# One turn of a background job placed 300 instructions ahead, Strassen sums on VectorE, and a planner's clock with new costs, in a hybrid decoder layer

## The chip, the cores and the metric

The kernel runs on one core of a Trainium2 chip. What counts is the device time of one execution in microseconds (us), as the median of several runs. Times inside the kernel come from one profiled execution.

## What is computed

One decoder layer on 1032 tokens (1024 of a prompt and 8 single ones of running sequences), width 1024, all in fp32:

```
x = x + 1/2 * SwiGLU_1(RMSNorm(x))                 # FFN1, inner width 2816
n = RMSNorm(x);  p = n @ w_in_mix                  # one projection, columns split among heads
mix = concat(window_attention(p), gated_DeltaNet(p)) @ w_out_mix
x = x + mix
x = x + 1/2 * SwiGLU_2(RMSNorm(x))                 # FFN2
y = RMSNorm(x)
```

`swiglu(x, w_in, w_out)` is `(silu(gate) * up) @ w_out`, with gate and up the two halves of `x @ w_in`. The DeltaNet group has four heads; each needs, in chunks of tokens, the inverse of a unit lower triangular matrix, and then a scan over the chunks that carries a state of 128 x 128. New caches and states are outputs beside `y`.

## The kernel before

The activations lie with the model's width on partitions: 8 tiles (`KT`) of 128 rows by 1032 tokens. TensorE (PE) multiplies in a fast format, so every fp32 product is three: high part by high part, high by low, low by high. A weight or an activation is split into `hi` (a cast on ScalarE, ACT) and `lo` (a subtraction on VectorE, DVE, or on GpSimd, POOL). `mm3` (L325 to L327) is one such triple. Tokens go in three chunks of 344, or in four quarters of `HW` = 258; two quarters make a half `p`.

**Stages.** *FFN in* uses a Strassen-like scheme: `w_ops` and `x_ops` build seven weight and seven activation operands out of four blocks by sums and differences, and `product` (L515 to L517) multiplies each pair into one of three PSUM banks. `x_ops` makes four 128x1032 sums (`t1`, `t2`, and two in place in `x`) and splits seven operands into `xhi` and `xlo`. The first `HEAD` = 4 column blocks f of FFN1 are done by `ffn_head` without that scheme, out of the raw x times the norm's gain (`xg`): there 1/rms (`rs`) of each token is multiplied in when the two PSUM banks are evacuated, so PE can start before the norm is known. *FFN out* (`ffn_out`) is plain `mm3`. The *token mix* (`mix_in`, `mix_out`) projects, convolves, does attention and DeltaNet, and ends in the product with `w_out_mix` in two passes, the second of which adds into x, squares and feeds the norm of FFN2.

**Norms.** `prepare(p, ...)` handles a half: `squares` (FFN1), then `rstd`, which lets PE sum over partitions (rows `ones,acc`), does a reciprocal square root by an integer guess and three Newton steps in small DVE operations (`nv`, `rsqt`, `rsqy`), spreads the result on a diagonal (`t`, three DVE operations) and lets PE broadcast it (rows `t,ones`); then 8 norm products on DVE per quarter (SCALAR_TENSOR_TENSOR `x<-x,c_norm_g,ps`), and `x_ops`.

**Order.** PE executes exactly in the order in which the program emits its instructions. On the other engines a scheduler decides the order, by each instruction's place in the program as its priority. The program is one main thread plus background jobs: generators in `Net.bg`, each advanced by `tick`, which `mm3` and `product` call after their three matmuls with a planned duration. `Net.now` is the planner's clock; `book` estimates when an instruction of a job will be done, from a fixed part and a rate per element of its engine (`Timed`) and a hop `HOP_NS` between instructions; a job goes on when `job.at <= now`. So the planner's numbers set where a job's PE instructions stand among the main products. A job yields a positive number (wait until its own last instruction is ready, and that much longer), or a negative one (look again that much later).

**Memory.** 44 SBUF slots of 128 x 1060 words hold nearly everything; `reserve` takes 8 of them for streamed weights: two raw, six for split pairs, so three weight tiles are live at a time (`issue`, `take`, `drop`). PSUM has 3 `mm` and 5 `ps` banks.

**DeltaNet of head h.** An inverse is a chain of 62 DVE operations on `Tb` and `inv`. The result is written to DRAM and read back in another layout (`scr_t`, `mg`, on SyncE's queue SP), copied on ACT (`mg<-mg`) and then used by PE (`mg,NT`). The helper through which DVE, ACT and POOL operations are recorded is L89, the DMAs' is L102, PE's small products are L247 and its transposes L252.

## Time and profile before

| | |
|---|---|
| median of 3 runs | 2123.35 us (2121.09 to 2125.12) |
| the profiled execution | 2120.43 us, of it 2118.7 us span |
| TensorE clock granted in it, mean | 0.962 |
| PE busy | 2016.0 us (95%) |
| DVE busy | 1187.5 us (56%) |
| ACT busy | 673.7 us (32%) |
| POOL busy | 597.4 us (28%) |

PE is busy all the time from about 150 to 750 us (FFN1) and from 1450 to 2100 us (FFN2 and the last norm). It idles at the start (loads and the first norm), in the token mix (about 750 to 1340 us) and around the start of FFN2 (1340 to 1445 us). A table by stretches gives busy time and number of instructions of PE, PEld (weight load), DVE, ACT and POOL, the granted clock (1.00 is full), the busy share of the DMA engines and GB/s. A row of a timeline gives start, duration, engine, line, operation, output<-inputs, shape and count; several alike in a row are one line, and in brackets stands the idle time ahead of it and what ended that.

### The profile page before, as it was taken

To read this page: it belongs to the slowest core of one execution; us is meant where nothing else is said; L and a number is where in the kernel's file an instruction comes from. 1 tells how busy PE (TensorE), PEld (TensorE's weight loads), DVE (VectorE), ACT (ScalarE), POOL (GpSimd) and SP (SyncE) were. 2 spreads that over 40 slices of the span, in tenths; PEclk is the share of its full clock that TensorE was granted. 3 is DMA by queue.
4 is the path that set the end of the run, shared out by engine and by line. 5 is a ranking of instruction groups with operands and counts; after the bars stand their busy time and mean duration, and the time that the engine had idled before them with its cause. 6 is when DMAs were issued, how large, how long until landed. Compare 5 with 4: busy or idle time off the path is not lost.

```text
span 2118.7 us, 37131 instructions
## 1 busy us (share of the span) xinstructions
PE 2016.0 (95%) x14990; PEld 1964.4 (93%) x14990; DVE 1187.5 (56%) x2634; ACT 673.7 (32%) x1463; POOL 597.4 (28%) x539
## 2 busy tenths in 40 slices
PE   7899999999999999999898988969999999999997
PEld 6899999999999998879788978869999999999997
DVE  7665444446433545786778865775444444464335
ACT  5233323333111324563332422333323333331112
POOL 2544434431000132330211212454444434200003
PEclk8999999999999999998989989979999999999998
DMA  4212222227321221222112261203222222552112
GB/s 149 66 62 94 77 85 72 80 81 283 100 78 51 96 77 45 58 76 64 47 51 54 71 224 57 98 21 99 71 81 81 81 81 79 181 208 78 56 40 81
DMA packets 115293, 187.16 MB, mean 88 GB/s; under 512 B 36080, under 2 KB 67216, under 8 KB 115104
## 3 DMA queue, kind: packets, MB, share of 16 engines
q1 hardware_dynamic: 113360, 178.41, 26.4%
q0 software_dynamic: 1760, 6.37, 0.8%
q8 instruction: 117, 1.92, 0.4%
q14 instruction: 56, 0.46, 0.1%
HBM read 138.77 MB, written 47.02 MB: 88 GB/s over the span
## 4 chain that ended last, share of the span: by engine, by line
PE 77%; DVE 11%; DMA 2%; issue 1%; ACT 1%; SPq 1%; POOL 0%; DVEq 0%; ACTq 0%; POOLq 0%
PE mm L325 11%; PE mm L326 11%; PE mm L327 10%; PE ps L515 9%; PE ps L516 9%; PE ps L517 9%; PE ps L247 5%; PE mm L516 4%; PE mm L515 4%; PE mm L517 4%; DVE conv L89 1%; DVE inv L89 1%; PE ps L252 1%; DVE x L89 1%; DVE xlo L89 1%
## 5 line engine op out<-in xcount | busy, mean ns | idle before, releaser
L515 PE MATMUL ps<-xhi,wop 128*128 128x258 f32 x1600 | 456.2, 285 | 7.0 <-DVE sw L89 2.9
L516 PE MATMUL ps<-xlo,wop 128*128 128x258 f32 x1600 | 454.6, 284 | 5.5 <-DVE xlo L89 5.5
L517 PE MATMUL ps<-xhi,wop 128*128 128x258 f32 x1600 | 454.4, 284 | 0.0
L325 PE MATMUL mm<-hhi,hi 128*128 128x344 f32 x1008 | 322.6, 320 | 0.0
L326 PE MATMUL mm<-hlo,hi 128*128 128x344 f32 x1008 | 322.2, 320 | 0.0
L327 PE MATMUL mm<-hhi,lo 128*128 128x344 f32 x1008 | 322.0, 319 | 0.0
L515 PEld LDWEIGHTS ps<-xhi,wop 128*128 128x128 f32 x1600 | 304.8, 191 | 8.4 <-DVE sw L89 3.7
L516 PEld LDWEIGHTS ps<-xlo,wop 128*128 128x128 f32 x1600 | 305.8, 191 | 6.1 <-DVE xlo L89 6.1
L517 PEld LDWEIGHTS ps<-xhi,wop 128*128 128x128 f32 x1600 | 304.9, 191 | 0.0
L89 DVE TENSOR_TENSOR wop<-r,wop 128x512 fp32r<-128x512 f32 x200 | 156.0, 795 | 196.7 <-ACT wop L89 178.4
L89 DVE SCALAR_TENSOR_TENSOR x<-mm,x 128x344 f32<-128x344 f32 x240 | 123.3, 515 | 220.9 <-PE mm L327 219.5
L516 PE MATMUL mm<-xlo,wop 128*128 128x258 f32 x640 | 182.2, 285 | 9.0 <-DVE xlo L89 9.0
L327 PEld LDWEIGHTS mm<-hhi,lo 128*128 128x128 f32 x1008 | 189.5, 188 | 0.0
L326 PEld LDWEIGHTS mm<-hlo,hi 128*128 128x128 f32 x1008 | 189.4, 188 | 0.0
L325 PEld LDWEIGHTS mm<-hhi,hi 128*128 128x128 f32 x1008 | 189.3, 188 | 0.0
L89 ACT CAST hi<-raw 128x1024 fp32r<-128x1024 f32 (+2 forms) x79 | 76.2, 965 | 336.3 <-PE mm L326 302.6
L515 PE MATMUL mm<-xhi,wop 128*128 128x258 f32 x640 | 182.0, 284 | 0.0
L517 PE MATMUL mm<-xhi,wop 128*128 128x258 f32 x640 | 181.7, 284 | 0.0
L89 POOL TENSOR_TENSOR acc<-acc,t 128x344 f32<-128x344 f32 (+1 forms) x50 | 47.1, 942 | 473.9 <-ACT t L89 464.2
L89 ACT CAST wop<-r 128x512 fp32r<-128x512 f32 x200 | 120.6, 620 | 181.5 <-DMA r<-in_w_in 132.5
L325 PE MATMUL mm<-xnhi,hi 128*128 128x344 f32 x488 | 173.0, 355 | 0.0
L89 POOL TENSOR_TENSOR ws<-r 128x512 f32<-128x512 f32 x40 | 52.3, 1307 | 402.4 <-DMA r<-in_w_in 375.4
(341 smaller groups left out, 4406.1 us busy)
## 6 DMA issues: line engine op xcount, KB each, us to landing
r<-in_w_in SPq DMA_DIRECT2D x86, 512.0 KB, 3.6
hraw<-hd SPq DMA_DIRECT2D x44, 516.0 KB, 4.9
hd<-sw SPq DMA_DIRECT2D x80, 258.0 KB, 2.0
raw<-in_w_out SPq DMA_DIRECT2D x32, 512.0 KB, 3.7
raw<-in_w_mix SPq DMA_DIRECT2D x22, 512.0 KB, 3.7
x<-in_x SPq DMA_DIRECT2D x16, 516.0 KB, 8.9
raw<-in_w_out SPq DMA_DIRECT2D x20, 384.0 KB, 3.2
xd<-x SPq DMA_DIRECT2D x24, 172.0 KB, 1.9
```

What stands on the lines that cost most here:

```text
L89: return fn(out, *a, **k)
L247: self.nc.tensor.matmul(out, lhsT, rhs, start=start, stop=stop, skip_group_check=pair is not None)
L252: self.nc.tensor.transpose(out, x, self.ident[:p, :p])
L325: mm(ps, whi, xhi, start=start, stop=False)
L326: mm(ps, whi, xlo, start=False, stop=False)
L327: mm(ps, wlo, xhi, start=False, stop=stop)
L515: mm(ps, w[:, a], x[0][:, c], start=first, stop=False, skip_group_check=True)
L516: mm(ps, w[:, a], x[1][:, c], start=False, stop=False, skip_group_check=True)
L517: mm(ps, wlo, x[0][:, c], start=False, stop=last, skip_group_check=True)
```

## The change

1. *Priority.* Each turn of a background job is emitted under a priority 300 instructions ahead of its place (`HOT`). On PE the order stays that of the program.
2. *Planner.* The hop after an instruction depends on its engine (260 DVE, 200 ACT, 260 POOL instead of 130), or is 70 if the same engine follows itself; PE counts 220 instead of 150, rates and the planned time of a triple change a little. A job that yields `None` goes on `LEAD` = 1200 ns before its last instruction is planned to be done. Norm products yield after each, `x_ops` after each operand.
3. *Sums.* The sums of `squares` and `x_ops` go to DVE for FFN1's first half and for FFN2, and stay on POOL for FFN1's second half. In the second pass of `w_out_mix` all sums of squares go to POOL (before, two of eight were on DVE).
4. *Weight slots.* Two live weight tiles instead of three; where a group needs all of its tiles at once, one more is held in plain slots.
5. *First head block.* For f = 0 the two banks of each quarter are copied by ACT into two `early` tiles at once; a job `first` multiplies by `rs`, does Silu and product later, with one store.

DVE has 2439 rows after for 2442 before, ACT 1204 for 1198, POOL 503 for 512; PE has the same 13522.

```diff
-WSLOTS = 8
+WSLOTS = 6
+LIVE = 2
+HOT = 300
...
-PE_NS = 150.0
-HOP_NS = 130.0
+PE_NS = 220.0
+LEAD = 1200.0
+SELF_HOP = 70.0
...
-        self.vector = Timed(net, nc.vector, 70.0, 1.04)
-        self.scalar = Timed(net, nc.scalar, 95.0, 0.83)
-        self.gpsimd = Timed(net, nc.gpsimd, 150.0, 2.1)
+        self.vector = Timed(net, nc.vector, 65.0, 1.05, 260.0)
+        self.scalar = Timed(net, nc.scalar, 185.0, 0.83, 200.0)
+        self.gpsimd = Timed(net, nc.gpsimd, 150.0, 2.1, 260.0)
...
-        ready = max(cur.ready, self.now + PE_NS)
+        ready = max(cur.last[1] + SELF_HOP if cur.last[0] is eng else cur.ready, self.now + PE_NS)
...
-        cur.ready = end + HOP_NS
+        cur.last = eng, end
+        cur.ready = end + eng.hop
...
-                    lat = next(job.gen)
-                    job.at = self.now - lat if lat < 0 else max(job.ready, self.now) + lat
+                    with self.tc.high_priority(HOT):
+                        lat = next(job.gen)
+                    if lat is None:
+                        job.at = max(job.ready - LEAD, self.now)
+                    else:
+                        job.at = self.now - lat if lat < 0 else max(job.ready, self.now) + lat
...
-        self.now += 15.0 if pair else max(110.0, n * 4 / 2.4)
+        self.now += 15.0 if pair else max(222.0 if lhsT.shape[0] == P else 60.0, n * 4 / 2.4)
...
-        for _ in range(3):
+        for _ in range(LIVE):
...
-        while self.plan and self.live < 3:
+        while self.plan and self.live < LIVE:
...
-        self.tick(int(xhi.shape[1]) * 3 / 2.36)
+        self.tick(27.0 + int(xhi.shape[1]) * 1.29)
...
-    def square(self, acc, k, x, pool=False):
+    def square(self, acc, k, x, pool=False, dve=DVE_SQ):
...
-    def x_ops(self, blk, n, out, keep=0):
-
-        tt = self.nc.gpsimd.tensor_tensor
+    def x_ops(self, blk, n, out, keep, eng):
+
+        tt = eng.tensor_tensor
...
-            self.tick(HW * 3 / 2.2)
+            self.tick(27.0 + HW * 1.29)
...
+        def first():
+            while len(done) < 4:
+                yield -300.0
+            for t in early:
+                nc.vector.tensor_tensor(t, t, rs, ALU.mult)
+            nc.scalar.activation(early[0], early[0], AF.Silu)
+            nc.gpsimd.tensor_tensor(early[1], early[1], early[0], ALU.mult)
+            nc.sync.dma_start(hd[:, 0, :], early[1])
+            self.fr(*early)
+            yield PAD
+
+        early = [self.bt(s="early") for _ in range(2)]
...
-                self.due.append((lambda p=p, l=l: (p, l) in done, partial(evac, f, c, *ps)))
-                self.settle_rs(2 if f == 0 else 1)
+                if f:
+                    self.due.append((lambda p=p, l=l: (p, l) in done, partial(evac, f, c, *ps)))
+                    self.settle_rs(1)
+                else:
+                    for t, o in zip(early, ps):
+                        nc.scalar.copy(t[:, c * HW:(c + 1) * HW], o)
...
+            if f == 0:
+                late = self.spawn(first())
...
+        self.wait(late)
...
-            nc.gpsimd.tensor_tensor(a, a, b, ALU.add)
+            eng.tensor_tensor(a, a, b, ALU.add)
...
                 nc.vector.scalar_tensor_tensor(y, y, self.norm_g[:, gi, k:k + 1], bcs[:, :w], ALU.mult, ALU.mult)
+                yield None
...
-        for ok in self.x_ops([xs[0][0], xs[0][1], xs[1][0], xs[1][1]], 4 * HW, out, 3 if sq is not None else 0):
-            yield -300.0 if ok else -500.0
+        for ok in self.x_ops([xs[0][0], xs[0][1], xs[1][0], xs[1][1]], 4 * HW, out, 3 if sq is not None else 0, eng):
+            yield None if ok else -500.0
...
-                        self.square(acc[:, c % 2 * HW:(c % 2 + 1) * HW], m, at(m, c))
+                        self.square(acc[:, c % 2 * HW:(c % 2 + 1) * HW], m, at(m, c), dve=())
...
-            n.spawn(n.prepare(p, xs[p], n.bt(s="acc"), 0, xT[p], rs, done, xg["ready"]))
+            n.spawn(n.prepare(p, xs[p], n.bt(s="acc"), 0, xT[p], (n.nc.vector, n.nc.gpsimd)[p], rs, done, xg["ready"]))
...
-            n.spawn(n.prepare(p, x, acc, 2, xT[p]))
+            n.spawn(n.prepare(p, x, acc, 2, xT[p], n.nc.vector))
```

**The order at the start of FFN2.** These are the sums of the first half's operands (`t1`, `t2`, `x`) on POOL before, with a sum of squares of the second half among them:

```order
L89 TENSOR_TENSOR t1_2127_14693<-x_1867_13191,x_1866_13189 128x1032
L89 TENSOR_TENSOR t2_2128_14694<-x_1967_13691,t1_2127_14693 128x1032
L89 TENSOR_TENSOR x_1867_13191<-x_1967_13691,x_1867_13191 128x1032
L89 TENSOR_TENSOR acc_2077_14417<-acc_2077_14417,t2_2134_14726 128x258
L89 TENSOR_TENSOR x_1966_13689<-x_1966_13689,t2_2128_14694 128x1032
```

And these rows stand on DVE now, at the same place in the program (`nv`, `rsqt` and `rsqy` are the first small steps of the second half's norm):

```order
L92 TENSOR_TENSOR t1_2133_14746<-x_1869_13204,x_1868_13202 128x1032
L92 TENSOR_SCALAR nv_2138_14758<-ps_2137_14757 86x6
L92 TENSOR_TENSOR xlo_2156_14892<-x_1969_13708,xhi_2155_14891 128x1032
L92 TENSOR_TENSOR t2_2134_14747<-x_1969_13708,t1_2133_14746 128x1032
L92 TENSOR_SCALAR rsqt_2140_14767<-nv_2138_14758 86x6
L92 TENSOR_TENSOR x_1869_13204<-x_1969_13708,x_1869_13204 128x1032
L92 TENSOR_TENSOR xlo_2145_14796<-t1_2133_14746,xhi_2144_14795 128x1032
L92 TENSOR_TENSOR x_1968_13706<-x_1968_13706,t2_2134_14747 128x1032
L92 TENSOR_SCALAR rsqy_2139_14766<-rsqt_2140_14767 86x6
L92 TENSOR_TENSOR xlo_2148_14819<-t2_2134_14747,xhi_2147_14818 128x1032
L92 TENSOR_TENSOR xlo_2153_14865<-x_1869_13204,xhi_2152_14864 128x1032
```

The four sums moved from POOL to DVE, in between the `xlo` that depend on them, and a norm's chain stands among them. On PE the `ones,acc` rows of the second half stand after 7731 main matmuls, before after 7857.

**The order of the second norm at the start.** DVE before, the end of the chain for the second half (its result `t2` is the first row of the last three):

```order
L89 SCALAR_TENSOR_TENSOR x_6_102<-x_6_102,c_norm_g_74,ps_71_562 128x258 x2
L89 SCALAR_TENSOR_TENSOR rsqy_68_539<-rsqt_69_540,rsqy_68_539 86x6
L89 SCALAR_TENSOR_TENSOR x_6_102<-x_6_102,c_norm_g_74,ps_71_562 128x258 x2
L89 SCALAR_TENSOR_TENSOR x_8_106<-x_8_106,c_norm_g_74,ps_71_562 128x258 x4
L89 TENSOR_TENSOR rsqt_69_540<-rsqy_68_539 86x6
L89 SCALAR_TENSOR_TENSOR rsqt_69_540<-rsqt_69_540,nv_67_531 86x6
L89 SCALAR_TENSOR_TENSOR rsqy_68_539<-rsqt_69_540,rsqy_68_539 86x6
L89 TENSOR_SCALAR t2_70_552<-ident_125,rsqy_68_539 86x86 x3
L89 TENSOR_TENSOR t2_76_583<-ps_47_292,rs_32_179 128x258
L89 TENSOR_TENSOR t2_77_584<-mm_48_293,rs_32_179 128x258
L89 TENSOR_SCALAR t2_93_658<-ident_125,rsqy_68_539 86x86 x3
L89 TENSOR_TENSOR xlo_81_596<-t1_72_575,xhi_80_595 128x1032
```

DVE now, the same chain, behind the 8 norm products of the first half (`t1`, `t2_90`, `x_6`, `x_7` are its sums):

```order
L92 TENSOR_TENSOR t1_89_731<-x_6_102,x_5_100 128x1032
L92 SCALAR_TENSOR_TENSOR rsqy_80_655<-rsqt_81_656,rsqy_80_655 86x6
L92 TENSOR_TENSOR t2_90_732<-x_8_106,t1_89_731 128x1032
L92 TENSOR_TENSOR x_6_102<-x_8_106,x_6_102 128x1032
L92 TENSOR_TENSOR rsqt_81_656<-rsqy_80_655 86x6
L92 TENSOR_TENSOR xlo_98_793<-t1_89_731,xhi_97_792 128x1032
L92 SCALAR_TENSOR_TENSOR rsqt_81_656<-rsqt_81_656,nv_79_647 86x6
L92 TENSOR_TENSOR xlo_101_829<-t2_90_732,xhi_100_828 128x1032
L92 TENSOR_TENSOR xlo_106_867<-x_7_104,xhi_105_866 128x1032
L92 SCALAR_TENSOR_TENSOR rsqy_80_655<-rsqt_81_656,rsqy_80_655 86x6
L92 TENSOR_TENSOR x_7_104<-x_7_104,t2_90_732 128x1032
L92 TENSOR_SCALAR t2_82_668<-ident_125,rsqy_80_655 86x86 x3
```

The norm products were there before; the sums and three `xlo` now stand ahead of the end of the chain, too. On PE its `ones,acc` row stands after 276 main matmuls (before 186), and the first row that needs its end after 300 (before 219).

**The order at the last DeltaNet head.** The end of the inverse on DVE before:

```order
L89 TENSOR_TENSOR inv_1764_12748<-bd_1733_12644,Tb_1734_12655 128x16
L89 SCALAR_TENSOR_TENSOR t2_1846_13114<-ps_1845_13109,c_gdn_g_148,z_1691_12416 128x512
L89 TENSOR_TENSOR Tb_1734_12655<-Tb_1734_12655,inv_1764_12748 128x16
L89 SCALAR_TENSOR_TENSOR S_1848_13123<-S_1834_13065,g_gle_8734,ps_1847_13121 128x128
L89 TENSOR_TENSOR inv_1765_12751<-bd_1733_12644,Tb_1734_12655 128x8
L89 TENSOR_TENSOR Tb_1734_12655<-Tb_1734_12655,inv_1765_12751 128x8
```

The same end now:

```order
L92 TENSOR_TENSOR inv_1776_12811<-bd_1746_12710,Tb_1747_12721 128x24
L92 TENSOR_TENSOR Tb_1747_12721<-Tb_1747_12721,inv_1776_12811 128x24
L92 TENSOR_TENSOR inv_1777_12814<-bd_1746_12710,Tb_1747_12721 128x16
L92 TENSOR_TENSOR Tb_1747_12721<-Tb_1747_12721,inv_1777_12814 128x16
L92 TENSOR_TENSOR x_1868_13202<-mm_1872_13210,x_1868_13202 128x258
L92 TENSOR_TENSOR inv_1778_12817<-bd_1746_12710,Tb_1747_12721 128x8
L92 TENSOR_TENSOR Tb_1747_12721<-Tb_1747_12721,inv_1778_12817 128x8
```

Now `x<-mm_1872`, a residual sum that waits for a main product of PE, stands ahead of the last two rows of the inverse. On PE, from behind that product's last matmul (`mm_1872`) to the use of `mg`, there are the 15 matmuls of `mm_1875`, and then these rows:

```order
L333 MATMUL mm_1880_13269<-m_1817_12990,hi_1803_12944 128x258
L334 MATMUL mm_1880_13269<-m_1818_12991,hi_1803_12944 128x258
L335 MATMUL mm_1880_13269<-m_1817_12990,lo_1804_12945 128x258
L255 MATMUL ps_1881_13273<-kn_1856_13157,st_1842_13098 128x1 x8
L333 MATMUL mm_1880_13269<-m_1821_13012,hi_1803_12944 128x258
L334 MATMUL mm_1880_13269<-m_1822_13013,hi_1803_12944 128x258
L335 MATMUL mm_1880_13269<-m_1821_13012,lo_1804_12945 128x258
L255 MATMUL ps_1884_13292<-mg_1779_12824,NT_1738_12675 32x32 x16
L260 MATMUL ps_1885_13311<-ident_125,dl_1882_13282 8x128
```

That makes 21 main matmuls; before there were 90 between the matmul that the end of the inverse stood behind (`ps_1847`) and this use.

37 lines of the change are left out of this document (20 added, 17 removed).

## The prediction

> **What bounds the kernel now.** The page's head and its fourth part come first. The fourth part follows the work that ended last.
>
> ```profile
> span 2118.7 us, 37131 instructions
> PE 2016.0 (95%) x14990; PEld 1964.4 (93%) x14990; DVE 1187.5 (56%) x2634; ACT 673.7 (32%) x1463; POOL 597.4 (28%) x539
> PE 77%; DVE 11%; DMA 2%; issue 1%; ACT 1%; SPq 1%; POOL 0%; DVEq 0%; ACTq 0%; POOLq 0%
> ```
>
> PE sets the end: 95% busy, and no other engine comes near. The change leaves PE's work alone, so it can only take from the 2118.7 − 2016.0 = 103 us of idle PE and from time at a lower clock. The table of stretches says where those lie (columns after the stretch: its length, busy time and instructions of each engine, PE's granted clock, DMA).
>
> ```profile
> 0.00:41.00 41.00, 29.18 (x180) 27.47 (x180) 28.43 (x51) 26.38 (x49) 11.79 (x11) 0.79 0.58 192
> 41.00:72.00 31.00, 20.11 (x131) 19.76 (x132) 27.93 (x71) 9.62 (x13) 14.44 (x6) 0.78 0.03 9
> 72.00:122.00 50.00, 50.00 (x419) 50.00 (x419) 22.78 (x40) 12.00 (x21) 22.36 (x16) 1.00 0.30 91
> 550.00:600.00 50.00, 50.00 (x320) 50.00 (x319) 24.38 (x37) 10.71 (x11) 0.00 (x0) 1.00 0.31 100
> 900.00:1340.00 440.00, 399.77 (x2977) 368.61 (x2976) 318.99 (x1003) 160.76 (x460) 81.72 (x66) 0.91 0.27 81
> 1340.00:1375.00 35.00, 31.48 (x248) 30.66 (x247) 27.84 (x68) 12.98 (x30) 17.23 (x21) 0.95 0.30 103
> 1375.00:1445.00 70.00, 49.93 (x352) 48.06 (x351) 54.47 (x79) 23.29 (x36) 36.97 (x19) 0.80 0.13 39
> 1450.00:1500.00 50.00, 50.00 (x418) 50.00 (x418) 23.73 (x44) 15.88 (x34) 23.88 (x21) 1.00 0.25 83
> ```
>
> An undisturbed stretch issues 418 matmuls of 258 columns in 50 us, 0.120 us each, or 320 of 344 columns, 0.156 us each. Against that pace 41 to 72 us (the first norm) holds 131 × 0.120 = 15.7 us of work and loses 15; 1375 to 1445 us (the start of the second feed-forward, FFN2) holds 352 × 0.120 = 42 us and loses 28; 1340 to 1375 loses 35 − 248 × 0.120 = 5. The token mix, 900 to 1340, is idle for 440 − 399.8 = 40 us and runs at clock 0.91, some 0.09 × 440 = 40 us more. The change aims at these three places. The stalls themselves, by what PE waits for (total us, times, longest):
>
> ```profile
> PE mm L516 <- DVE xlo L89: 9.0, 2, 5.4
> PE ps L247 <- ACT w L89: 8.8, 2, 5.6
> PE mm L325 <- DVE t L89: 8.0, 2, 7.8
> PE ps L516 <- DVE xlo L89: 5.5, 2, 5.1
> ```
>
> **The change part by part.**
>
> **Sums of the Strassen operands go from POOL to DVE** (all of them for FFN2, half for FFN1). These are the DVE, POOL and PE rows at the worst place of FFN2's start (start, duration, engine, instruction, count):
>
> ```profile
> 1417.21 5.43 DVE L89 TENSOR_TENSOR xlo<-x,xhi 128x1032 fp32r<-128x1032 f32 x2
> 1422.57 6.74 DVE L89 TENSOR_TENSOR xlo<-t,xhi 128x1032 fp32r<-128x1032 f32 x2
> 1415.86 2.36 POOL L89 TENSOR_TENSOR t<-x,x 128x1032 f32<-128x1032 f32 x1 [4.35 <-DVE x L89]
> 1418.30 3.25 POOL L89 TENSOR_TENSOR t<-x,t 128x1032 f32<-128x1032 f32 x1
> 1421.51 3.35 POOL L89 TENSOR_TENSOR x<-x,x 128x1032 f32<-128x1032 f32 x1
> 1419.37 0.58 PE L516 MATMUL ps<-xlo,wop 128*128 128x258 f32 x1 [5.08 <-DVE xlo L89]
> L89 DVE TENSOR_TENSOR xlo<-x,xhi x20: 1216/1222/3420, 49.3 to 1432.2; 128x1032 fp32r<-128x1032 f32 x20
> ```
>
> One `xlo` takes 1.22 us (median of 20). Beside a POOL sum it takes up to 3.42, and the sum takes 3.3 where 2.36 is its time with less beside it. So four `xlo` take 5.43 + 6.74 = 12.2 us where 4.9 would do, and PE waits behind them. On DVE the four sums cost 4 × 1.22 = 4.9 us, and sums and `xlo` together take 8 × 1.22 = 9.8 us, 2.4 less than now for one half of the tokens. The chain sum → cast → `xlo` also shortens: a sum is ready after 1.22, not 3.3 us. The Trainium skill (SBUF — State Buffer, "Who interferes with whom") says that a DVE instruction with two SBUF inputs and a GpSimd instruction that reads SBUF exclude each other for a whole instruction; that would make a pair 1.22 + 2.36 = 3.6 us, and the 3.3 to 3.4 here nearly agree. By the page the change has a price too: it puts all square sums of the last `w_out_mix` pass on POOL, where each would block DVE in turn. That adds 2 of 8 per quarter, some 1 us, and I leave it out of the sum.
>
> The second gain at FFN2 is place. In the order of PE the second half's norm (the `ones,acc` row) moves some 126 products forward, so its chain runs beside the first half's products, 126 × 0.120 = 15 us of cover. The stretch loses 28 + 5 = 33 us now. I expect two waits of about 3 us for the norms, about 3 for the first operands, and with them about 8 us at the lower clock: 17 left, a gain of **16**. Bounds: 6 (only the two `xlo` rows, 9.0 + 5.5, go, and 8 comes back as waits for the earlier norm) and 25 (only one chain is left).
>
> **First norm.** PE's long wait is for an evacuation queued behind a norm chain that POOL stretches:
>
> ```profile
> 68.60 3.22 DVE L89 SCALAR_TENSOR_TENSOR x<-x,c_norm_g,ps 128x258 f32<-128x258 f32 x8
> 58.95 2.37 POOL L89 TENSOR_TENSOR t<-x,t 128x1032 f32<-128x1032 f32 x1
> 61.29 2.35 POOL L89 TENSOR_TENSOR x<-x,x 128x1032 f32<-128x1032 f32 x1
> 59.13 2.22 DVE L89 SCALAR_TENSOR_TENSOR rsqy<-rsqt,rsqy 86x6 f32<-86x6 f32 x1
> 61.38 2.67 DVE L89 TENSOR_SCALAR t<-ident,rsqy 86x86 f32<-86x86 f32 x3
> 64.87 0.55 PE L325 MATMUL mm<-xghi,phi 128*128 128x258 f32 x1 [7.75 <-DVE t L89]
> 67.10 0.38 ACT L89 COPY rs<-ps 128x258 f32<-128x258 f32 x1 [1.25 <-PE ps L247]
> 1235.61 0.17 DVE L89 TENSOR_TENSOR rsqt<-rsqy 128x16 f32<-128x16 f32 x1
> ```
>
> A small operation of that chain takes 2.2 us there, and a like one 0.17 with POOL quiet. Eight ACT copies of 0.38 us now free the banks of f = 0 without waiting for the norm; that is 3.0 us on an engine busy 9.6 of 31. The later scaling, Silu and product (2 × 1.22 on DVE, one ACT pass, one POOL product) have the rest of the head as cover, and only a store hangs on them. Without that cover they would cost about 6 us. So the 7.75 us wait goes. But another comes: the second half's chain is now interleaved on DVE with 8 norm products (3.2 us for 8), 4 sums and 3 `xlo` (1.22 each) and some 12 small steps (0.2 each), 3.2 + 8.5 + 2.4 = 14 us, and PE has 24 matmuls, 2.9 us, between the `ones,acc` rows that start this chain and the row that needs its end. A stall of about 11 us stands there. From 41 to 72 us PE is idle for 31 − 20.1 = 10.9 us now, so the idle time only changes its name. What is gained: the squares of the first half are added on DVE (two sums of 1.22 us for POOL's 2.36 and more, about 2 us on the chain ahead of the first norm), and one long stall instead of two brings the lower clock once, about 3 of the 0.22 × 31 = 6.8 us. Together **5**. Bounds: 0 (nothing but the name changes) and 12 (DVE does the small steps between its waits for ACT's casts, and the stall is half as long).
>
> **Token mix.** `HOT` and the new planner costs move DVE, ACT and PE rows by some tens of places each way; most of this I cannot price. One place is plain: the last head's triangular inverse. Its result goes through two DMAs and an ACT copy (`mg`) before PE may go on:
>
> ```profile
> 1034.54 0.16 DVE L89 TENSOR_TENSOR Tb<-Tb,inv 128x8 f32<-128x8 f32 x1
> 1044.53 0.64 ACT L89 COPY mg<-mg 128x256 f32<-128x256 f32 x1 [8.52 <-DMA mg<-scr_t]
> 1227.36 0.17 DVE L89 TENSOR_TENSOR Tb<-Tb,inv 128x8 f32<-128x8 f32 x1
> 1249.91 0.64 ACT L89 COPY mg<-mg 128x256 f32<-128x256 f32 x1 [2.54 <-DMA mg<-scr_t]
> 1250.61 0.69 PE L247 MATMUL ps<-mg,NT 32*32 32x32 f32 x32 [2.55 <-ACT mg L89]
> 1250.00:1300.00 50.00, 49.10 (x412) 45.75 (x413) 25.13 (x75) 14.46 (x43) 5.18 (x4) 0.83 0.21 67
> ```
>
> From the last inverse row to the end of `mg` head 1 took 1044.53 + 0.64 − 1034.54 = 10.6 us and head 3 took 23.2. In the changed order of head 3 a residual sum that waits for a product of PE stands ahead of the last two inverse rows, and only 21 matmuls (2.5 us) and eight small ones lie between that product and `ps<-mg,NT`; before it was 90. So PE waits 10.6 − 2.5 − 0.5 = 7.6 us there, or 20 if the DMA queue is late again, where it waits 2.55 now: 5 to 18 worse. Against it stand longer planned hops (130 to 200–260 ns), which space the scan's steps 9 products apart instead of 6, and shorter stretches under POOL. I take **+5** for the mix, with −12 and +25 as ends: an end of −12 is a quarter of the idle and clock that is lost there beside what was priced, +25 is 18 and one more 7.
>
> **Two live weight tiles for three.** A tile of w_out lasts 72 × 0.156 = 11.2 us; its successor needs a DMA, a cast and a subtraction.
>
> ```profile
> raw<-in_w_out SPq DMA_DIRECT2D x32, 512.0 KB, 3.7
> L89 ACT CAST hi<-raw 128x1024 fp32r<-128x1024 f32 (+2 forms) x79 | 76.2, 965 | 336.3 <-PE mm L326 302.6
> ```
>
> That is 3.7 + 1.0 + 1.2 = 5.9 us, which the tile ahead covers: nothing. If a raised job delays the cast by more than 5 us, each of some 40 tiles would pay the rest.
>
> **Sum:** −5 − 16 + 5 = −16 us. The profiled execution took 2120.43 us (span 2118.7 and 1.7 around it), 2.9 under the median of 2123.35. Taken from the median: 2107; from the execution: 2104. I say 2106.
>
> **The rivals.**
>
> *The gain is larger (about 2078).* Only short stalls are left, and the clock stays full. In 1375 to 1445 the clock of 0.80 is 14 us of lost pace, and as much as 40 us in the mix. Head 12, FFN2 25 and a mix that gains 8 make −45. The Trainium skill's page (TensorE: Matmul & The Clock Gate, "What's actually happening") has half rate after about 3.4 us of idling only. By that page the waits of some 3 us that I leave at FFN2 would cost no clock. The row 1250 to 1300 speaks against a full recovery: only a stall of 2.55 us, and 49.1 of 50 us busy, yet clock 0.83.
>
> *No change (about 2122).* Stalls only change their names: head 0, FFN2 6, mix +5. What speaks for it is that two norm chains remain in each start and that DVE, not POOL, then carries everything: it is busy for 54.5 of 70 us at FFN2's start already. Against it: part of that is stretch, and 9.8 us of DVE work takes the place of 12.2.
>
> *Slower (about 2136): ACT is held at `mg` in the mix.* The copy stands 39 and 33 products earlier on ACT for heads 0 and 2, with attention exponentials and copies queued behind it that PE needs soon. ACT idled 8.52 us at such a copy in head 1, and PE then lost 5.6 (the row `ACT w`). Two more of these, 11, and head 3 with the late queue, 18, with 5 of lower clock, make +34 against gains of 21: +13. It decides as soon as the mix loses over 21. For it: the tight order of head 3, certain from the order. Against it: the queue was late in one head of the two shown.
>
> **How the numbers follow.** The forecast 0.53, larger 0.13, no change 0.13, slower 0.21. The forecast's own range is 2090 to 2117. The ends of the sum are 2123 − 12 − 25 − 12 = 2074 and 2123 − 0 − 6 + 25 = 2142; the range of 8 in 10 leaves out the outer part of the larger gain and of the slower case: 2080 to 2136. A difference under 0.2%, 4 us, cannot be told from none. Faster: 0.53 + 0.13 + 0.01 of the no-change case, 0.67. Same: 0.12. Slower: 0.21.
>
> **What would show it.** Right for FFN2: `xlo` at 1.22 us in its start, the waits for `xlo` under 4 us in all, and 70 us holding over 430 matmuls. Right for the head: no wait of 7.75 for `t` at f = 0 or 1, one of about 11 us some 55 to 68 us into the run, and full pace from there on. Right for the mix: `ps<-mg,NT` of the last head waits 7 to 8 us. The forecast is wrong if PE waits behind ACT at `mg` in three heads, if stretches that now show 50.00 busy show less (two live tiles are too few), or if the second norm chain at FFN2 stalls PE as long as the `xlo` rows do now.

## The result

| | before | after |
|---|---|---|
| median of 7 runs | 2122.21 us (2117.09 to 2125.12) | 2132.51 us (2129.39 to 2138.42) |
| the profiled execution | 2120.43, of it 2118.7 span | 2129.39, of it 2127.5 span |
| TensorE clock granted in it | 0.962 | 0.960 |

The change makes the kernel slower: the ratio after to before is 1.0050, with a 95% interval of 1.0036 to 1.0063. The forecast was 2106 us. The head of the profile of after, and the line of its fourth part by engine:

```profile
span 2127.5 us, 37082 instructions
PE 2008.6 (94%) x14990; PEld 1962.5 (92%) x14990; DVE 1188.8 (56%) x2634; ACT 678.1 (32%) x1468; POOL 564.1 (27%) x530
PE 80%; DVE 13%; DMA 3%; ACT 2%; issue 2%; SPq 1%; POOL 0%; DVEq 0%; ACTq 0%; POOLq 0%
```

PE has as many instructions as before and is busy for 7.4 us less, so its idle time inside the span grew from 102.7 to 118.9 us. DVE's share of the chain that ended last rose from 11 to 13%, DMA's from 2 to 3%.

Stretches of equal time compare badly once the two kernels are shifted against each other. All kernels here issue the same 13056 main matmuls (of 258 or 344 columns) in the same order, so I compare the start of the Nth of them. (The places named ahead of the result leave out 48 matmuls with 16 columns of weights, so from the 5712th on they are 48 lower than here.) This table is my own count from the traces of one profiled execution each; times in us. The head of the program ends before the 1000th, FFN1 runs steadily to the 5200th, the token mix lies between the 5200th and the 7400th, FFN2's start from there to the 8200th, and "tail" is what follows the 12900th.

```
               to 1000  1000-5200  5200-7400  7400-8200  8200-12900  tail   PE ends
before           168.0      557.1      597.8      135.7       618.4  33.9    2110.9
after            171.3      557.0      601.5      134.8       618.5  36.2    2119.3
after - before    +3.4       -0.1       +3.7       -0.9        +0.1  +2.3      +8.4
```

The steady stages did not move. The head lost 3.4 us, the mix 3.7, the tail 2.3, and FFN2's start, where the forecast's gain was to come from, gained 0.9. These are small differences: the kernels below that keep the order of PE's instructions of after in a stage reach 168.6 to 171.3 at the 1000th, 601.5 to 608.6 in the mix and 131.8 to 138.4 at FFN2's start. Now the table of stretches and the waits of PE (total us, times, longest) of after:

```profile
41.00:72.00 31.00, 22.25 (x174) 21.87 (x172) 18.31 (x53) 7.65 (x11) 0.81 (x1) 0.89 0.06 22
72.00:122.00 50.00, 45.10 (x357) 45.10 (x358) 30.67 (x56) 14.23 (x24) 15.38 (x13) 0.90 0.23 72
900.00:1340.00 440.00, 386.65 (x2940) 360.11 (x2937) 313.93 (x972) 156.74 (x452) 84.55 (x65) 0.91 0.26 76
1340.00:1375.00 35.00, 28.26 (x212) 27.43 (x212) 24.50 (x50) 14.09 (x31) 20.58 (x22) 0.90 0.35 118
1375.00:1445.00 70.00, 56.38 (x409) 55.02 (x410) 54.98 (x104) 25.16 (x39) 14.86 (x17) 0.83 0.13 46
```

```profile
PE ps L255 <- DVE t L92: 24.0, 7, 9.8
PE ps L255 <- ACT mg L92: 15.1, 1, 15.1
PE ps L525 <- DVE sw L92: 5.2, 4, 1.9
PE mm L335 <- DVE wlo L92: 4.7, 1, 4.7
PE mm L526 <- DVE xlo L92: 3.0, 1, 3.0
PE ps L525 <- ACT sw L92: 3.0, 1, 3.0
PE ps L255 <- ACT w L92: 2.7, 2, 1.4
```

Each place that the prediction spoke of looks better in one stretch and worse in the next: 41 to 72 us holds 43 more matmuls, 72 to 122 us 62 fewer; 1375 to 1445 holds 57 more, 1340 to 1375 36 fewer. The old waits (for `w` 8.8, for `t` in front of `mm` 8.0, for `xlo` 9.0 and 5.5) are gone or down to 2.7 and 3.0. New ones stand in their place: for the diagonal `t` of a norm, for `mg`, for `wlo`.

**Where the head lost its gain.** The 240th matmul starts 14.0 us earlier than before, at 58.1 us instead of 72.1; the 300th is only 1.2 us ahead, the 390th 1.2 us behind. Between the 240th and the 300th lies PE's longest wait for `t`, up to 76.9 us. DVE's rows of after ahead of it:

```profile
64.63 0.16 DVE L92 TENSOR_TENSOR rsqt<-rsqy 86x6 f32<-86x6 f32 x1
64.96 1.66 DVE L92 SCALAR_TENSOR_TENSOR x<-x,c_norm_g,ps 128x258 f32<-128x258 f32 x4 [0.17 <-ACT rs L92]
66.55 0.15 DVE L92 SCALAR_TENSOR_TENSOR rsqt<-rsqt,nv 86x6 f32<-86x6 f32 x1
...
68.19 1.22 DVE L92 TENSOR_TENSOR t<-x,x 128x1032 f32<-128x1032 f32 x1
69.34 0.15 DVE L92 SCALAR_TENSOR_TENSOR rsqy<-rsqt,rsqy 86x6 f32<-86x6 f32 x1
...
75.33 0.15 DVE L92 SCALAR_TENSOR_TENSOR rsqy<-rsqt,rsqy 86x6 f32<-86x6 f32 x1
75.44 1.23 DVE L92 TENSOR_TENSOR x<-x,t 128x1032 f32<-128x1032 f32 x1
76.59 0.60 DVE L92 TENSOR_SCALAR t<-ident,rsqy 86x86 f32<-86x86 f32 x3
```

The second half's norm is a chain of small steps of 0.15 us, and the first half's norm products, sums and `xlo` stand between them. The chain's `nv` started at 63.45, so `t` was 13.1 us later.

A second loss follows. The sums of FFN1's second half stayed on POOL, and they stretch `xlo` as before (DVE, then POOL):

```profile
124.07 6.88 DVE L92 TENSOR_TENSOR xlo<-x,xhi 128x1032 fp32r<-128x1032 f32 x2 [1.03 <-PE mm L335]
126.53 3.34 POOL L92 TENSOR_TENSOR x<-x,x 128x1032 f32<-128x1032 f32 x1
```

Two `xlo` take 6.88 us where 2.4 would do without POOL beside them. At 144 us PE waits 3.0 for `ACT sw`, and from the 390th to the 1000th after loses another 2.2 us on before.

**Head 3 of the mix.** DVE's last inverse row, ACT's copy and PE's row behind it, then the DMAs issued from 1238 to 1254 us (KB each, median us from issue to landing), then the stretches around them:

```profile
1237.21 0.17 DVE L92 TENSOR_TENSOR Tb<-Tb,inv 128x8 f32<-128x8 f32 x1
1252.75 0.64 ACT L92 COPY mg<-mg 128x256 f32<-128x256 f32 x1 [16.31 <-DMA mg<-scr_t]
1253.45 1.06 PE L255 MATMUL ps<-mg,NT 32*32 32x32 f32 x32 [15.10 <-ACT mg L92]
```

```profile
scr_t<-Tb SPq DMA_DIRECT2D x4, 32.0 KB, 6.0
mg<-scr_t SPq DMA_DIRECT2D x4, 32.0 KB, 1.8
```

```profile
1231.00:1240.00 9.00, 5.99 (x40) 5.49 (x38) 6.37 (x48) 1.14 (x4) 0.22 (x1) 0.76 1.10 366
1240.00:1246.00 6.00, 0.00 (x0) 0.00 (x0) 0.00 (x0) 0.00 (x0) 0.00 (x0) 0.50 0.97 273
1246.00:1252.00 6.00, 0.00 (x0) 0.00 (x0) 0.27 (x1) 0.00 (x0) 0.00 (x0) 0.50 0.30 32
```

From the inverse to `mg` pass 16.2 us. From 1240 to 1252 nearly nothing runs on the compute engines; the DMA engines are full up to 1246 and 0.30 busy after that. Before, the same way took 23.2 us, but 90 main products of PE covered it and PE waited 2.6.

**FFN2's start.** DVE's rows of after, from a weight split that PE waits 4.7 us for, and then from the second half's norm, with PE's row that needs its end:

```profile
1349.75 1.70 DVE L92 TENSOR_TENSOR wop<-ws,wop 128x512 fp32r<-128x512 f32 x1
...
1351.70 1.14 DVE L92 TENSOR_TENSOR wlo<-raw,whi 128x768 fp32r<-128x768 f32 x1
...
1393.52 0.15 DVE L92 TENSOR_SCALAR nv<-ps 86x6 f32<-86x6 f32 x1
1393.63 1.23 DVE L92 TENSOR_TENSOR xlo<-x,xhi 128x1032 fp32r<-128x1032 f32 x1
1394.79 1.23 DVE L92 TENSOR_TENSOR t<-x,t 128x1032 f32<-128x1032 f32 x1
1395.93 0.16 DVE L92 TENSOR_SCALAR rsqt<-nv 86x6 int32<-86x6 int32 x1
...
1399.43 0.16 DVE L92 TENSOR_SCALAR rsqy<-rsqt 86x6 int32<-86x6 int32 x1
...
1404.98 0.61 DVE L92 TENSOR_SCALAR t<-ident,rsqy 86x86 f32<-86x86 f32 x3
1405.39 0.70 PE L255 MATMUL ps<-t,ones 86*128 86x86 f32 x2 [4.23 <-DVE t L92]
```

`xlo` does take 1.23 us now, not 3.4. But the norm that was moved forward meets the first half's sums and `xlo` on DVE: from `nv` to `t` it takes 11.5 us, 3.1 before. On PE only 21 main products stand between the `ones,acc` rows that start this chain (they end at 1391.6) and the row that needs its end (1405.39). The waits of PE there, one by one, are 4.7 (`wlo`), 1.6 (`t`), 1.1 (`acc`), 2.1 (`xhi`), 3.0 (`xlo`), 4.2 (`t`), and 1.9, 1.3 and 1.7 (`sw`): 21.6 us. Three of them, `xhi`, `xlo` and the second `t`, 9.3 us together, lie between those two rows.

### The profile page after: what moved, and what is told of

It is laid out like the page before. It is cut to its first block, busy times and chain, and to the rows that moved or that the text cites. A ratio compares the mean times of both kernels' runs of the same rounds, so it can differ in the third digit from the quotient of the medians.

```text
span 2127.5 us, 37082 instructions
## 1 busy us (share of the span) xinstructions
PE 2008.6 (94%) x14990; PEld 1962.5 (92%) x14990; DVE 1188.8 (56%) x2634; ACT 678.1 (32%) x1468; POOL 564.1 (27%) x530
## 4 chain that ended last, share of the span: by engine, by line
PE 80%; DVE 13%; DMA 3%; ACT 2%; issue 2%; SPq 1%; POOL 0%; DVEq 0%; ACTq 0%; POOLq 0%
PE mm L333 11%; PE mm L335 11%; PE mm L334 11%; PE ps L525 9%; PE ps L527 9%; PE ps L526 9%; PE ps L255 5%; PE mm L525 3%; PE mm L527 3%; PE mm L526 3%; DVE conv L92 2%; DVE x L92 1%; PE ps L260 1%; SPq L105 1%; DVE rsqt L92 1%
## 5 line engine op out<-in xcount | busy, mean ns | idle before, releaser
L333 PE MATMUL mm<-hhi,hi 128*128 128x344 f32 x960 | 307.0, 320 | 0.0
L335 PE MATMUL mm<-hhi,lo 128*128 128x344 f32 x960 | 306.7, 320 | 0.0
L334 PE MATMUL mm<-hlo,hi 128*128 128x344 f32 x960 | 306.6, 319 | 0.0
L334 PEld LDWEIGHTS mm<-hlo,hi 128*128 128x128 f32 x960 | 180.4, 188 | 0.0
L335 PEld LDWEIGHTS mm<-hhi,lo 128*128 128x128 f32 x960 | 180.4, 188 | 0.0
L333 PEld LDWEIGHTS mm<-hhi,hi 128*128 128x128 f32 x960 | 180.4, 188 | 0.0
L92 POOL TENSOR_TENSOR acc<-acc,t 128x344 f32<-128x344 f32 (+1 forms) x58 | 51.8, 893 | 478.4 <-ACT t L92 475.0
L92 DVE TENSOR_TENSOR sw<-ps,sw 128x258 f32<-128x258 f32 x240 | 101.1, 424 | 123.8 <-PE ps L527 122.6
```

The lines of the kernel that those rows point to most:

```text
L92: return fn(out, *a, **k)
L333: mm(ps, whi, xhi, start=start, stop=False)
L334: mm(ps, whi, xlo, start=False, stop=False)
L335: mm(ps, wlo, xhi, start=False, stop=stop)
```

## The experiments

The theory after this comparison: the gains at the head and at FFN2 are there, but are given back because the norm's chain of small steps now stands among sums and `xlo` on one engine, with a late weight split and a late `mg` beside it. The rivals: the priority pulls the wrong work forward; the planner's new costs put PE's small products in worse places; the queue in front of the stores is the whole wait of head 3.

"1000th" and the stages are those of the table above; all ratios are to the kernel before, from runs on the same chip.

**The norm chain in the head.** The edit makes the first half's sums wait for the second half's reciprocal root, so that they can't stand inside its chain. The wait is made by data: a column of ones that is computed out of the root (root times 0 plus 1) multiplies one operand of the first sum.

```diff
+            nc.vector.memset(g, 1.0)
+            nc.vector.tensor_scalar(g[:m], r[:, 0:1], 0.0, 1.0, ALU.mult, ALU.add)
...
-        tt(t1, b12, b11, ALU.subtract)
+        if gate:
+            eng.scalar_tensor_tensor(t1, b12, gate[0][:, 0:1], b11, ALU.mult, ALU.subtract)
```

> The changed kernel with one data dependence more: in FFN1's start the first difference of the first half reads a column of ones that is made from the end of the second half's reciprocal square root, so that the sums and xlo on DVE cannot stand among its small steps. Theory A (the 9.85 us wait for t at 77 us is the norm chain stretched by sums and xlo in its gaps): the chain shrinks from 13.1 us to about 6.5 (8 norm products stay in it), the wait falls to 3 to 4 us, the 390th main matmul starts 6 to 9 us earlier than the 91.4 us of the changed kernel, and the total falls by as much, to about 2125. Rival B (the work itself is the bound there, the order only names it): the wait moves to the first Strassen products, whose operands come 7 us later, and the total stays within 2 us of 2132.5.

Measured: 2127.99 us, ratio 1.0038 [1.0025, 1.0051]; after itself stands at 1.0050. The waits of PE in this run:

```profile
PE ps L255 <- DVE t L92: 15.5, 7, 4.2
PE ps L531 <- ACT sw L92: 8.2, 2, 7.4
```

The wait of 9.8 us for `t` is down to 1.9, the chain from `nv` to `t` to 5.6 us, and the 390th matmul starts at 79.4 us, 12.0 earlier than after. So it was the interleaved chain. But of the 12 us only 7.5 are left at the 1000th (163.8): the wait for `ACT sw` at 136 us grew from 3.0 to 7.4. The stretched `xlo` of the second half was late next.

**Both causes in the head.** The same edit, and the second half's sums on DVE as well:

```diff
-            n.spawn(n.prepare(p, xs[p], n.bt(s="acc"), 0, xT[p], (n.nc.vector, n.nc.gpsimd)[p], rs, done, xg["ready"]))
+            n.spawn(n.prepare(p, xs[p], n.bt(s="acc"), 0, xT[p], n.nc.vector, rs, done, xg["ready"]))
```

> The kernel e1 (with the dependence on the second half's norm) with the sums of FFN1's second half on DVE as well, none on POOL. Theory A (the 7.4 us wait for sw at 136 us in e1 is ACT standing behind casts whose xlo and sums stretch each other on DVE and POOL): the wait falls below 3 us, the 1000th main matmul starts at 155 to 159 us (163.8 in e1, 171.3 in the changed kernel, 168.0 before), the total falls by 5 to 8 against e1, to about 2121. Rival B (DVE is then the bound of the start): the wait moves to xlo, and the 1000th starts after 162 us.

Measured: 2107.82 us, ratio 0.9931 [0.9906, 0.9955]. The 1000th starts at 147.0 us, 24.3 earlier than after, and the wait for `ACT sw` is gone; `mg` (15.1) and `wlo` (4.7) stay. With chain and sums put right together the head is faster than before, too (168.0).

**The head's part alone, in the kernel before.** Into before go the early copies of f = 0, FFN1's sums on DVE and the column of ones, nothing else (`first` is true for FFN1):

```diff
-            nc.gpsimd.tensor_tensor(a, a, b, ALU.add)
+            (nc.vector if eng is None else eng).tensor_tensor(a, a, b, ALU.add)
...
-        for ok in self.x_ops([xs[0][0], xs[0][1], xs[1][0], xs[1][1]], 4 * HW, out, 3 if sq is not None else 0):
+        for ok in self.x_ops([xs[0][0], xs[0][1], xs[1][0], xs[1][1]], 4 * HW, out, 3 if first else 0, self.gate if first and not p else None, nc.vector if first else None):
```

> The kernel before with three things in FFN1's start: the early ACT copies of f = 0, all FFN1 sums on DVE, and the dependence of e1; the order of PE from the token mix on is that of before. Theory A (the start alone is worth it once the chain is not stretched): the 1000th main matmul starts at 154 to 160 us for 168.0, nothing later changes by more than 3 us, the total falls by 8 to 13 to about 2110. Rival B (what is gained at the start is lost at another place of it): the 1000th starts after 164 us, the total within 4 us of before.

Measured: 2101.98 us, ratio 0.9902 [0.9882, 0.9921]. The 1000th starts at 150.0 us, 18.0 earlier than before; the rest of the stages stays within 1.5 us of before (599.2, 135.7, 618.8, 33.7).

**The early copies alone, in the kernel before.** With the job `first` as in the change:

```diff
-                self.due.append((lambda p=p, l=l: (p, l) in done, partial(evac, f, c, *ps)))
-                self.settle_rs(2 if f == 0 else 1)
+                if f:
+                    self.due.append((lambda p=p, l=l: (p, l) in done, partial(evac, f, c, *ps)))
+                    self.settle_rs(1)
+                else:
+                    for t, o in zip(early, ps):
+                        nc.scalar.copy(t[:, c * HW:(c + 1) * HW], o)
```

> The kernel before with the early ACT copies of f = 0 alone; sums stay on POOL. Theory A (the early copies are most of the gain at the start; sums on DVE add the rest): the 1000th main matmul starts at 157 to 163 us (168.0 before, 150.0 in e7), nothing changes later, the total is 5 to 11 below before. Rival B (without sums on DVE the norm chain is stretched by POOL as before and PE waits for it): the 1000th starts after 165 us, total within 3 us of before.

Measured: 2114.63 us, ratio 0.9966 [0.9946, 0.9985]. The 1000th starts at 160.1, 7.9 earlier. The copies pay by themselves; the other 10 us of the run above come with sums and chain. The sums of `x_ops` on DVE alone (a run further below) bring 1.3 us there.

**The priority.** In after:

```diff
-HOT = 300
+HOT = 0
```

> The changed kernel with HOT = 0; PE's order is the same. Theory A (the loss is in the sums on DVE, the planner's places and the two live tiles, not in the priority): the three big waits (t 9.85, mg 15.1, wlo 4.7) stay within 2 us each and the total within 5 us of 2132.5. Rival B (raised jobs push the main thread's rows back): waits on rows of the main thread (wlo, sw, x) vanish, and the total falls below 2124.

Measured: 2132.72 us, ratio 1.0059 [1.0044, 1.0074], with the waits of after (`mg` 16.1, `wlo` 4.7):

```profile
PE ps L255 <- DVE t L92: 23.6, 7, 9.8
```

The 300 instructions of priority, the words by which the change is named, do nothing to the total that can be measured.

**The planner's costs, both ways.** First the old costs in after (`PE_NS`, hops, rates and planned times; the rest of the change stays):

```diff
-PE_NS = 220.0
+PE_NS = 150.0
...
-SELF_HOP = 70.0
+HOP_NS = 130.0
...
-        self.vector = Timed(net, nc.vector, 65.0, 1.05, 260.0)
-        self.scalar = Timed(net, nc.scalar, 185.0, 0.83, 200.0)
+        self.vector = Timed(net, nc.vector, 70.0, 1.04, 130.0)
+        self.scalar = Timed(net, nc.scalar, 95.0, 0.83, 130.0)
...
```

> The changed kernel with all planner costs of before (PE 150, hop 130 everywhere, rates, planned times of a triple); priority, sums on DVE, two live tiles and early copies stay. The use of mg of head 3 then stands after main matmul 7050, not 6996. Theory A (the new hop of 70 ns after an instruction of the same engine plans the 62 steps of the inverse too short, and so PE comes to mg too early): the 15.1 us wait for mg falls below 9, main matmuls 7000 to 7400 take 95 to 99 us for the 102.9 of the changed kernel and the 95.2 of before, and the total falls by 4 to 8, to about 2126. Rival B (the DMA engines are full there and the place does not matter): the wait stays over 12 us, or another of the same size takes its place, and the stretch over 101 us.

Measured: 2105.26 us, ratio 0.9913 [0.9892, 0.9934], so some 27 us below after by the medians, where 4 to 8 were expected, and 21 by the profiled executions. The second half's norm of the head stands in one piece on DVE; the last two rows are from FFN2's start:

```profile
55.56 0.16 DVE L92 TENSOR_SCALAR nv<-ps 86x6 f32<-86x6 f32 x1
...
57.89 0.17 DVE L92 SCALAR_TENSOR_TENSOR rsqy<-rsqt,rsqy 86x6 f32<-86x6 f32 x1
58.09 1.14 DVE L92 TENSOR_SCALAR t<-ident,rsqy 86x86 f32<-86x86 f32 x6
...
1377.92 0.15 DVE L92 TENSOR_SCALAR nv<-ps 86x6 f32<-86x6 f32 x1
...
1389.04 1.14 DVE L92 TENSOR_SCALAR t<-ident,rsqy 86x86 f32<-86x86 f32 x6
```

In the head it takes 2.5 us to the start of `t`, not 13.1; the 1000th starts at 153.1 us, 18.2 earlier than after. The wait for `mg` falls to 5.5, as expected, and the tail to 33.7 us. FFN2's start takes 129.5, 5.3 less than in after, although the chain there is as interleaved as in after (11.1 us from `nv` to `t`) and PE waits 11.9 us for `t`, in one stretch; the last section comes back to that. The mix, at 607.1 us, is worse than in after (601.5).

Then the new costs alone in before, the same lines the other way round:

> The kernel before with the new planner costs alone. Theory A (the planner's costs alone lose time in the mix): main matmuls 5200 to 7400 take 5 to 15 us more than the 597.8 of before, the start and FFN2's start stay within 3 us, the total is 2126 to 2136. Rival B (they do harm only with two live tiles and raised jobs): the mix stays within 4 us of before, and so does the total.

Measured: 2146.01 us, ratio 1.0105 [1.0085, 1.0125]: the head +4.2, the mix 615.1 (+17.3, more than expected), FFN2's start +1.2, the tail 35.9 (+2.0). The costs alone lose some 24 us (23 by the medians, 24.5 by the stages), where a total of 2126 to 2136 was expected. They are the largest loss among the parts tried alone; the early copies, the sums and the two tiles each leave the mix within 3.2 us of before and the tail within 0.8.

**Two live weight tiles, both ways.** Three tiles and eight slots in after:

```diff
-WSLOTS = 6
-LIVE = 2
+WSLOTS = 8
+LIVE = 3
```

> The changed kernel with three live weight tiles and 8 weight slots again. Theory A (the 4.7 us wait for wlo at the start of FFN2 is the cost of two live tiles: the last tile is split late, behind raised jobs on DVE): no wait for wlo or lo over 1 us is left, and the stretch from main matmul 7500 to 7600 takes 4 to 5 us less than the 20.4 us of the changed kernel; the steady stages stay as they are. The total moves by that and by what the mix's changed order brings, between 2118 and 2134. Rival B (the wait is DVE's, not the tile's): a wait of 3 us or more for DVE stays in that stretch.

Measured: 2136.78 us, ratio 1.0080 [1.0057, 1.0103]. The wait for `wlo` is gone, and the 100 matmuls around it (7500th to 7600th) take 15.0 us instead of 20.4: that price is real, 5.4 us. But on PE the mix has another order (the use of `mg` of head 3 stands 33 main matmuls later) and takes 612.1 us, 10.6 more than after, so the total is no better (expected 2118 to 2134). Two tiles in before (`WSLOTS = 6`, `LIVE = 2`, the rest as it was):

> The kernel before with two live weight tiles alone (6 slots, one tile more in plain slots where a group is held). Theory A: a wait of 4 to 5 us for wlo appears between main matmuls 7500 and 7600, steady stages stay as they are, the mix moves by less than 5 us, the total is 2124 to 2131. Rival B (the late split needs raised jobs or sums on DVE ahead of it): no wait for wlo over 1 us, total within 3 us of before.

Measured: 2127.61 us, ratio 1.0014 [0.9997, 1.0030]; its runs went from 2116.07 to 2132.70, and the profiled one was the fastest. In it a wait for `wlo` of 4.4 us appears that before doesn't have (7500th to 7600th: 19.0 us for 16.1), and the mix of this fast execution is 3.2 us shorter. In total no difference can be told.

**The queue in front of head 3's inverse.** The eight loads `x<-xd` of 516 KB move from SP's queue to POOL's.

```diff
-                            self.x_blocks(lambda kh, c0: xd[:, 4 * kh:4 * kh + 4, c0:c0 + HW], p, x[p], (m // 3,))
+                            self.x_blocks(lambda kh, c0: xd[:, 4 * kh:4 * kh + 4, c0:c0 + HW], p, x[p], (m // 3,), nc.swq)
```

> The changed kernel with the 8 loads of x in the first pass of w_out_mix (4 MB) issued on POOL's queue, not on SP's. Theory A (the 15.1 us wait for mg of head 3 is half the two hops through DRAM and half SP's queue, in which the loads of x stand ahead of the store of the inverse): from the last inverse row to mg it takes 10 to 11 us for 15.5, the wait falls to 7 to 9, the total by 6 to 9 us, to about 2125. Rival B (the transfers themselves share the 16 DMA engines, whoever issues them): the wait stays over 13 us, the total within 3 us of 2132.5.

Measured: 2129.01 us, ratio 1.0046 [1.0028, 1.0063]. The wait for `mg` and the stores ahead of it (issued from 1238 to 1256 us):

```profile
PE ps L256 <- ACT mg L92: 12.5, 1, 12.5
...
scr_t<-Tb SPq DMA_DIRECT2D x4, 32.0 KB, 4.8
```

The wait shrank by 2.6 us only, to a value between the two expectations (7 to 9, or over 13), and the stores still take 4.8 us to land, where the median of the whole run of after is 2.8. The queue was a small part of it. The DMA engines remain nearly as full up to 1246 us (share 1.05 and 0.89 in two stretches, 1.10 and 0.97 in after), so I put the rest down to the transfers sharing these engines; fewer bytes were not tried.

**All sums on DVE, and nothing else, in before.**

```diff
-        tt = self.nc.gpsimd.tensor_tensor
+        tt = self.nc.vector.tensor_tensor
```

> The kernel before with all sums of x_ops on DVE and nothing else. Theory A (sums on DVE pay where no norm chain runs beside them, as at FFN2's start in the places of before, where the second half's norm comes 126 products later): the xlo waits of 14.5 us fall below 5, main matmuls 7400 to 8200 take 126 to 130 us for 135.7, and the total falls by 4 to 10. Rival B (the sums stretch the norm chains as in the changed kernel): the waits for t grow by what the waits for xlo lose, and the stretch stays over 133 us.

Measured: 2118.19 us, ratio 0.9973 [0.9960, 0.9986]. The waits of PE:

```profile
PE mm L325 <- ACT t L89: 9.3, 1, 9.3
PE mm L516 <- DVE xlo L89: 6.9, 2, 5.0
PE ps L516 <- DVE xlo L89: 4.2, 1, 4.2
```

FFN2's start takes 133.6 us, 2.1 less, where 126 to 130 was expected. The waits for `xlo` only fell from 14.5 to 11.1, and one of 2.8 us for `t` came. Each `xlo` takes 1.22 us there, but 16 norm products of 6.39 us together stand on DVE ahead of the one that PE waits 4.2 us for: what is left is more the order of the work on DVE than its speed.

**A version with the parts that pay.** To the run with the head's part (before's planner and three live tiles) come: FFN2's sums on DVE, the squares of the last `w_out_mix` pass on POOL, and `x_ops` going on 1200 ns ahead as in the change.

```diff
-                    job.at = self.now - lat if lat < 0 else max(job.ready, self.now) + lat
+                    if lat is None:
+                        job.at = max(job.ready - 1200.0, self.now)
+                    else:
+                        job.at = self.now - lat if lat < 0 else max(job.ready, self.now) + lat
...
-            yield -300.0 if ok else -500.0
+            yield None if ok else -500.0
...
-                        self.square(acc[:, c % 2 * HW:(c % 2 + 1) * HW], m, at(m, c))
+                        self.square(acc[:, c % 2 * HW:(c % 2 + 1) * HW], m, at(m, c), dve=())
```

> The kernel e7 (before with the three edits of FFN1's start) and for FFN2: all sums on DVE, all sums of squares of the last pass on POOL, and x_ops goes on 1200 ns before its last instruction is planned to be done (as in the changed kernel); planner costs, priority and weight slots are those of before. On DVE the second half's norm chain then stands in one piece behind the first half's sums and xlo, and on PE its ones,acc rows come after main matmul 7758. Theory A (FFN2's start lost its gain in the changed kernel to a norm chain that sums and xlo stand in): main matmuls 7400 to 8200 take 118 to 124 us for 135.7 before and 134.8 in the changed kernel, waits for t and xlo there are under 5 us together, and the total is 10 to 16 below e7, near 2089. Rival B (DVE has too much to do there in any order): the stretch stays over 130 us, and the total within 5 us of e7's 2102.

Measured: **2093.24 us** (2090.29 to 2096.74), ratio 0.9857 [0.9838, 0.9875]. It beats both kernels. FFN2's start takes 122.3 us, 13.4 less than before. DVE's rows of the second half's norm there:

```profile
1378.33 0.14 DVE L89 TENSOR_SCALAR nv<-ps 86x6 f32<-86x6 f32 x1
...
1380.69 0.16 DVE L89 SCALAR_TENSOR_TENSOR rsqy<-rsqt,rsqy 86x6 f32<-86x6 f32 x1
1380.96 1.14 DVE L89 TENSOR_SCALAR t<-ident,rsqy 86x86 f32<-86x86 f32 x6
```

The chain takes 2.6 us to `t` instead of 11.5; only one evacuation stands inside it, and PE waits 1.1 us for it. The largest wait left there is 6.0 us for the first `xlo`, so that `t` and `xlo` miss the expected 5 us together, and the total is 8.7 below the run with the head's part, not 10 to 16. This run differs from after in the planner's costs, the priority and the live tiles too, so it shows that a gain is there when the chain stands in one piece, not which of these keeps it so, nor that the chain alone makes it.

## Why the prediction was wrong

**FFN2's start (forecast −16, measured −0.9): the step that failed.** Its first half held: `xlo` at 1.23 us, its waits 3.0 in place of 14.5, the `ones,acc` rows moved forward. The step that failed is the cover: "its chain runs beside the first half's products, 126 × 0.120 = 15 us of cover". The 126 products are how far the chain's start moved forward. What covers it are the products between its start and the row that needs its end, and these are 21 (39 before), 2.5 us at full pace, because that row moved forward with it. For the head the prediction had counted the same distance (24 matmuls) and the same interleaving (14 us); it did not carry them to FFN2. There the chain shares DVE with the first half's `xlo` and with sums that had just come from POOL, eight operations of 1.22 us between its `nv` and its `t`. From the end of the `ones,acc` rows to the row that needs `t` pass 13.8 us, in 9.3 of which PE waits.

In the terms of the sum: "two waits of about 3 us for the norms" came to 5.8, but that agreement is luck: on its way to the second `t` PE had already lost 5.1 us to the first operands ("about 3" in the sum), while the chain went on. Nothing stood in the sum for `acc` and `sw` (6.0; the `sw` are evacuations that stand behind norm products, sums and `xlo` on DVE) and for `wlo` (4.7). So PE's named waits were 21.6 us, not 9, and its whole idle time stayed about as it was (22.1 us for 23.6 before). The lower clock cost about 10 us, near the 8 that were said (half of 20.3 us of busy time at half rate). The prediction named a stall behind the second chain as a sign of being wrong, if it grew as long as that of the `xlo` rows. The size was not far off for a kernel whose chain stands in one piece: the combined version gains 13.4.

**Two live tiles (forecast 0): the step that failed beside it.** 5.9 us of DMA, cast and subtraction under 11.2 us of cover was the sum for a steady stage, where it held (557.0 us from the 1000th to the 5200th). At the start of FFN2 the subtraction `wlo` queues on DVE among splits of FFN2's weight operands, one of which takes 1.70 us: its cast is done at 1347.7 us and it starts at 1351.7, and PE waits 4.7 us. The way there and back shows it: 5.4 us less with three tiles, 2.9 more with two in before.

**Head (forecast −5, bounds −12 to 0; measured +3.4).** The stall stands at the place in the program that was named and takes 9.8 us where 11 were said, though it ends at 76.9 us, not by 68. Three things went otherwise than in the sum. The first is "about 2 us on the chain ahead of the first norm": the first half's squares are indeed ready at 35.9 us for 37.7 before, but PE's `ones,acc` rows now stand 21 main products later and start at 41.13 for 39.61. The second is "one long stall instead of two". A weight split (`plo`) stands on DVE among the first chain's steps and waits 3.6 us for its cast, so this chain takes 7.1 us from `nv` to `t`, 2.4 before, and PE still waits 3.8 us for its `t` at 49.65 us:

```profile
46.13 1.22 DVE L92 TENSOR_TENSOR plo<-r,phi 128x1024 fp32r<-128x1024 f32 x1 [3.59 <-ACT phi L92]
```

The third is the sums that stay on POOL for the second half, whose stretched `xlo` cost 3.0 us at 144; the prediction looked at the sums that move and not at those that stay. The reasoning also took the interleaved chain as given, which was the largest loss: with the chain freed of sums and `xlo`, and all sums on DVE, the 1000th matmul starts 24 us earlier.

**Token mix (forecast +5, measured +3.7).** Right in total, in part by luck: PE idles 13.9 us more there than before (55.5 for 41.6) and is busy for 10.2 us less with the same products, about half of it because less of its busy time ran at half rate (68.4 us for 79.6). The sum had neither. Head 3's wait is the one foreseen, 15.1 us between the 7.6 and the 20 given for a late queue; by the run with another queue the stores were slow beside the loads more than behind them. That the planner's costs alone lose 17.3 us here was within the end of +25, but the sum had no term for them.

**Tail (not in the sum, measured +2.3).** It comes with the new costs (35.9 in before with them, 33.7 in after without).

**Against the rivals.** The time is close to the slower rival's 2136, but only one term of it came: the wait at head 3's `mg`, 12.5 us more than before, where it had 18. PE did not wait behind ACT at `mg` of heads 0 and 2 (its waits for ACT's `w` fell from 8.8 to 2.7), and what decided was the gain that did not come. The nearest in kind is "stalls only change their names", which had FFN2 at −6. The step between 240th and 390th in the head is that case in one picture: 14 us gained, 15 given back.

On the shared port the Trainium skill (SBUF — State Buffer, "Who interferes with whom") and the trace nearly agree again: by its rule I estimate a pair of `xlo` and a POOL sum at 1.22 + 2.36 = 3.6 us, and the two at 124 us took 3.44 each.

**What stays open** is part of the mix. The planner's costs and the number of live tiles alone decided here where PE's small products stand in it, so the fourteen kernels have four orders (own count; us from the 5200th to the 7400th, in brackets PE's idle time in it):

```
                  three live tiles                two live tiles
costs of before   597.8 to 601.8 (41.0 to 43.8)   594.6, 607.1 (45.4, 46.1)
new costs         612.1, 615.1 (58.5, 52.0)       601.5 to 608.6 (53.0 to 55.5)
```

Two fields hold five kernels each, the others two. The new costs add some 7 to 17 us of idle time with either number of tiles, two tiles alone 2 to 5. The length adds up less well, as kernels of the same order differ by 3 to 13 us. Much of that is clock: the two at 594.6 and 607.1 us idle alike, but have 69.6 and 99.3 us of busy time at half rate. I can show the wait at `mg`, but not which small product causes the rest, nor why the clock differs between kernels of one order. One execution was profiled of each, so a difference of 3 us says little.

## What to carry to other kernels

Moving work off a slow engine, and a chain forward, gained nothing here while other work stood between the chain's small dependent steps on the same queue. Look at which instructions stand there, not only at busy time, and count as cover only the products between the row that starts a chain and the row that needs its end. Judge a change of several parts by its parts: here two of them (early copies, sums on DVE with the chain kept whole) gain about 1% together and a third (new planner costs) loses about 1% by itself. Comparing the start of the Nth matmul of a fixed sequence shows in one line where a gain was made and where it was given back.
